# Layer 0's 24 modulation chunks: from products on VectorE to products on TensorE, between the steps of the recurrences

## The chip, the cores and the metric

The kernel runs on one core of a Trainium2 chip. A core has TensorE (matrix products, written PE in the profile, with its weight loads PEld), VectorE (DVE), ScalarE (ACT), GpSimd (POOL) and SyncE (SP), which here issues nearly all transfers, each engine with a program of its own. The metric is the device time of one launch in microseconds; smaller is better.

## The reference

Two layers of a diffusion backbone work on 512 latent tokens of width 1024, with 256 context tokens in layer 0. Per layer, cut to what matters:

```
mod = silu(c) @ ada_w[layer] + ada_b[layer]          # 6 * 1024 values
sh_m, sc_m, gt_m, sh_f, sc_f, gt_f = split(mod, 6)
y = mixer(x * (1 + sc_m) + sh_m)
x = layernorm(4**0.25 * x + gt_m * y)
y = conv_ffn(x * (1 + sc_f) + sh_f)
x = layernorm(4**0.25 * x + gt_f * y)
```

Layer 0's mixer is a gated DeltaNet in both directions with four heads, beside four pooling groups; its results are concatenated and go through one output projection. `mod` is a product of one row with a wide matrix: 24 MB of weights per layer, each used once. Layer 0's `sh_m` and `sc_m` are needed for the first operation of all. The next three vectors, `gt_m`, `sh_f` and `sc_f`, are 3 x 1024 values, or 24 columns of 128: the 24 chunks of the title. They are needed by the output projection's residual (`gt_m`) and by the normalisation behind it (`sh_f`, `sc_f`).

## The kernel before, in words

Activations lie with features on the 128 partitions and tokens along the row. A product in full precision is made of three: weights and activations are split in a high and a low part (`piece`, lines 165 to 179: ScalarE writes `w_hi`, GpSimd or VectorE writes `w_lo`), and `gemm` (line 222) adds high x high, high x low and low x high. A planner fixes each engine's order of instructions ahead of the run, by priorities in program order and by its own estimate of times; an instruction marked `keep_in_program_order` keeps its place among those of its engine.

The first stage (`start`) makes `sh_m` and `sc_m` on TensorE: for each of four groups it loads eight tiles of weights of 128x512, multiplies each with two columns of `silu(c)` and `silu(c_ctx)` as the stationary operand (line 289), into one of four groups of 32 partitions, and turns the sums by four small products with `sel2` (line 311).

`even` then walks through a written plan of steps. `k`, `q` and `v` project keys, queries and values of a pair of heads; `e` sets up systems; `i0` solves the chunk inverses of pair 0, three chains at a time; `x0` runs the two directions of pair 0's recurrence together with the inverses of pair 1, four chains at a time; `r1` runs the recurrence of pair 1; `g`, `p` and `w` are the gates and pools, whose products fill TensorE between the steps of the chains; `d` ends the heads. `together` takes one step of every active chain in turn and may call a function after each turn. Projections take their results in four banks of PSUM (ring "0"), the chains' products in the other four (ring "1").

The 24 chunks are made on VectorE. `ada_rest` (lines 346 to 362) loads, for each column, 128 rows of the transposed weights in two halves of 128x512 (line 356), and multiplies each half with the row `silu(c)`, copied to all partitions, while it sums along the row (line 358). Twelve chunks are done in the turns of x0, eight in those of r1, and the last four in `out_proj`, by `between` (lines 1327 to 1331), one after each output tile; only then does `columns(0)` (line 1285) make the columns for the normalisation. The row of c is loaded and put through Silu once, in the first stage (lines 349 to 351). The feed-forward of layer 0 copies it into two banks (line 580) and makes the other 56 chunks by the same function; these stay as they are.

In `out_proj` the first three output tiles are made in halves of the contraction, as soon as their inputs are there. Tile 3 follows in one piece, and the last four (4 to 7) are made for one half of the tokens and then, in reverse, for the other, with the normalisation of the first half running beside the second.

## Time and profile before

| What | us |
|---|---|
| median of three runs | 1341.77 (1341.52 to 1342.78) |
| the profiled execution's own time | 1340.33 |
| its span | 1338.5 |
| TensorE busy (matmuls) | 1271.3 |
| TensorE busy (weight loads) | 1069.2 |
| VectorE busy | 907.3 |
| GpSimd busy | 680.5 |
| ScalarE busy | 583.9 |

The span runs from the first instruction of the program to the last. Times in the rows count from its start. A row of the timeline has start, duration, engine, line, operation, tiles and form; in square brackets stands how long the engine was idle before it and what ended that. A row of the stretches has the busy time of PE, PEld, DVE, ACT and POOL with the count of instructions, then the granted clock of TensorE as a share of full speed, the busy share of the transfer engines and GB/s. The chain of waits is followed back from the last instruction; its rows are start, duration and what held the time. A row of waits has who waited for whom, the sum in us, how often, and the longest.

### The profile page before, as it was taken

Reading aid. Unit: us, or ns where it says so; the run is one execution under the profiler, and the core shown is the slowest. Engines: PE = TensorE matmul, PEld = TensorE weight load, DVE = VectorE, ACT = ScalarE, POOL = GpSimd, SP = SyncE. Lnnn points to the kernel's source line nnn. Section 1 sums busy time; section 2 is a strip of 40 time slices with the busy share of each in tenths; the row PEclk is TensorE's granted clock in tenths of the full one; section 3 lists DMA queues with packets and bytes.
Section 4 is the critical chain, followed back from the end, with each engine's and each line's share of the span. In section 5 each row is a group of like instructions: output and inputs, shape, how many; then the busy total and the mean of one; then the engine's idle time right before and its main releaser. Section 6 shows DMA issues by size and latency. Waiting matters only on the chain.

```text
span 1338.5 us, 19585 instructions
## 1 busy us (share of the span) xinstructions
PE 1271.3 (95%) x6690; PEld 1069.2 (80%) x6690; DVE 907.3 (68%) x1865; ACT 583.9 (44%) x1091; POOL 680.5 (51%) x616
## 2 busy tenths in 40 slices
PE   6898899989889999999999999999999999999997
PEld 2587777878688888888888988778988888888886
DVE  3397899999776787788644668956676666661125
ACT  2355414445547433333322576545463334332235
POOL 1336447666445665555444566966143433443453
PEclk8899999999988999999999999999899999999998
DMA  9521221522523555656566432323123323333344
GB/s 302 201 87 46 42 60 53 166 83 87 173 81 105 163 189 190 198 194 196 185 206 195 141 111 87 95 87 107 35 95 99 98 95 96 101 91 96 93 123 126
DMA packets 104948, 166.59 MB, mean 124 GB/s; under 512 B 20944, under 2 KB 29200, under 8 KB 104848
## 3 DMA queue, kind: packets, MB, share of 16 engines
q1 hardware_dynamic: 93888, 164.09, 39.2%
q10 hardware_dynamic: 10960, 1.25, 0.7%
q8 instruction: 53, 0.87, 0.3%
q14 instruction: 47, 0.39, 0.1%
HBM read 162.60 MB, written 2.69 MB: 123 GB/s over the span
## 4 chain that ended last, share of the span: by engine, by line
PE 73%; DVE 11%; POOL 4%; issue 3%; ACT 2%; DMA 2%; SPq 0%; ACTq 0%; POOLq 0%; DVEq 0%
PE prod_ps L222 37%; PE out_ps L222 22%; PE half_ps L222 3%; DVE ada_w L358 2%; POOL w_lo L176 1%; PE qkv_ps L222 1%; POOL conf_far L1221 1%; PE ln_e L413 1%; PE it_ps L987 1%; PE gate_ps L222 1%; PE dd_ps L862 1%; DVE x_t L933 1%; DMA ada_w<-in_ada 1%; POOL cb_t L886 1%; PE ln_w L423 1%
## 5 line engine op out<-in xcount | busy, mean ns | idle before, releaser
L176 POOL TENSOR_TENSOR w_lo<-w_raw,w_hi 128x512 fp32r<-128x512 f32 (+1 forms) x299 | 385.0, 1292 | 449.8 <-ACT w_hi L170 441.5
L170 ACT CAST w_hi<-w_raw 128x512 fp32r<-128x512 f32 (+1 forms) x408 | 246.2, 608 | 454.1 <-PE out_ps L222 149.8
L222 PE MATMUL prod_ps<-uh,w_lo 128*128 128x512 f32 x792 | 308.9, 390 | 2.6 <-POOL w_lo L176 2.6
L222 PE MATMUL prod_ps<-uh,w_hi 128*128 128x512 f32 x792 | 308.7, 390 | 0.6 <-ACT w_hi L170 0.6
L222 PE MATMUL prod_ps<-ul,w_hi 128*128 128x512 f32 x792 | 308.4, 389 | 0.0
L601 DVE SCALAR_TENSOR_TENSOR f_acc<-prod_ps,prm,f_acc 128x441 f32<-128x441 f32 (+2 forms) x320 | 222.4, 695 | 60.1 <-ACT f_acc L590 50.8
L176 DVE TENSOR_TENSOR w_lo<-w_raw,w_hi 128x512 fp32r<-128x512 f32 (+1 forms) x109 | 87.0, 799 | 137.7 <-ACT w_hi L170 135.1
L222 PEld LDWEIGHTS prod_ps<-uh,w_lo 128*128 128x128 f32 x792 | 148.7, 188 | 35.2 <-POOL w_lo L176 4.3
L222 PEld LDWEIGHTS prod_ps<-uh,w_hi 128*128 128x128 f32 x792 | 148.8, 188 | 31.9 <-ACT w_hi L170 1.5
L222 PEld LDWEIGHTS prod_ps<-ul,w_hi 128*128 128x128 f32 x792 | 148.7, 188 | 30.4
L222 PE MATMUL out_ps<-ah,w_lo 128*128 128x256 f32 (+1 forms) x352 | 119.6, 340 | 5.6 <-DVE w_lo L176 5.6
L222 PE MATMUL out_ps<-ah,w_hi 128*128 128x256 f32 (+1 forms) x352 | 120.0, 341 | 4.6 <-ACT w_hi L170 2.9
L222 PE MATMUL out_ps<-al,w_hi 128*128 128x256 f32 (+1 forms) x352 | 120.5, 342 | 0.0
L222 PE MATMUL out_ps<-hl,w_hi 128*128 128x512 f32 (+1 forms) x280 | 98.3, 351 | 0.0
L222 PE MATMUL out_ps<-hh,w_hi 128*128 128x512 f32 (+1 forms) x280 | 98.0, 350 | 0.0
L222 PE MATMUL out_ps<-hh,w_lo 128*128 128x512 f32 (+1 forms) x280 | 98.0, 350 | 0.0
L222 PEld LDWEIGHTS out_ps<-ah,w_lo 128*128 128x128 f32 x352 | 68.4, 194 | 12.8 <-DVE w_lo L176 5.9
L222 PEld LDWEIGHTS out_ps<-ah,w_hi 128*128 128x128 f32 x352 | 68.5, 195 | 12.2 <-ACT w_hi L170 3.4
L358 DVE SCALAR_TENSOR_TENSOR ada_w<-ada_w,crow_ps 128x512 f32<-128x512 f32 x112 | 70.8, 683 | 8.7 <-DMA ada_w<-in_ada 8.7
L222 PEld LDWEIGHTS out_ps<-al,w_hi 128*128 128x128 f32 x352 | 68.5, 195 | 7.7 <-DVE al L453 0.8
L222 PEld LDWEIGHTS out_ps<-hl,w_hi 128*128 128x128 f32 x280 | 52.7, 188 | 7.7
L222 PEld LDWEIGHTS out_ps<-hh,w_lo 128*128 128x128 f32 x280 | 52.6, 188 | 7.7
(362 smaller groups left out, 2323.4 us busy)
## 6 DMA issues: line engine op xcount, KB each, us to landing
ada_w<-in_ada SPq DMA_DIRECT2D x192, 256.0 KB, 4.0
w_raw<-in_ffn_up SPq DMA_DIRECT2D x176, 256.0 KB, 2.6
w_raw<-in_ffn_down SPq DMA_DIRECT2D x100, 256.0 KB, 2.7
w_raw<-in_even_in SPq DMA_DIRECT2D x40, 256.0 KB, 2.9
w_raw<-in_odd_in SPq DMA_DIRECT2D x40, 256.0 KB, 2.7
w_raw<-in_even_out SPq DMA_DIRECT2D x16, 256.0 KB, 2.8
w_raw<-in_odd_out SPq DMA_DIRECT2D x16, 256.0 KB, 2.8
w_raw<-in_ffn_down SPq DMA_DIRECT2D x20, 128.0 KB, 2.1
```

What stands on the lines that cost most here:

```text
L170: r = nc.scalar.copy(out=hi[:, :n], in_=raw)
L176: r = eng.tensor_tensor(out=lo[:, :n], in0=raw, in1=hi[:, :n].bitcast(F32), op=SUB)
L222: r = nc.tensor.matmul(out=o, lhsT=w, rhs=x[k][:, c0:c1], start=clear and k == i == 0, stop=k == n - 1 and i == 2, skip_group_check=pin)
L358: r = nc.vector.scalar_tensor_tensor(out=w, in0=w, scalar=1.0, in1=c, op0=MUL, op1=MUL, accum_out=self.mod[:, k, i:i + 1])
L413: nc.tensor.matmul(out=pe[:, 2 * (n * e + i):2 * (n * e + i) + 2], lhsT=t[:, i * P:(i + 1) * P], rhs=ones, start=e == 0 and i == 0 and not ...
L423: nc.tensor.matmul(out=o, lhsT=self.ones, rhs=d[:, 0:n].rearrange("p a b -> p (a b)"), start=True, stop=True)
L601: nc.vector.scalar_tensor_tensor(out=o, in0=sv[:, r0 + dr:r1 + dr, q0 + dc:q1 + dc], scalar=w[:, tap:tap + 1], in1=o, op0=MUL, op1=ADD)
L862: nc.tensor.matmul(out=o, lhsT=self.tri[:, 2 + d], rhs=r, start=d == 0, stop=d == 1)
L886: nc.gpsimd.tensor_tensor(out=t, in0=m[:, 2 * c:2 * c + 2], in1=self.mask(self.blk, 2), op=MUL)
L933: nc.vector.tensor_tensor(out=t, in0=a2[w, :, r, r + 1:16][:, :, None, :].broadcast_to([96, 2, m, m]), in1=x[w, :, r + 1:16, r + 1:16].rea ...
L987: nc.tensor.matmul(out=pt[:, h], lhsT=m[:, h], rhs=r1[:, h], start=True, stop=True)
L1221: nc.gpsimd.tensor_tensor(out=far, in0=far, in1=f, op=ADD)
```

## The change

The 24 chunks are taken out of `ada_rest` and made on TensorE, as in the first stage. The weights for them are laid out in memory as six groups of 512 outputs, each with eight tiles of 128x512 for the contraction (`ada2`). A call of `ada_quad` loads four tiles and multiplies each with a stationary operand of six columns, of which one holds `silu(c)` and five are zero: group g's column stands at place g, so that all six groups add into the same bank, at rows 32q to 32q+5 for the tile's place q among four. Twelve calls make all sums. They are made at every third turn of the chains in i0, x0 and r1, each product kept at its place in TensorE's program. `ada_columns`, a new meaning of the step `a0`, which now stands before `w3 d0 w1 d1`, copies the bank to SBUF, turns and sums it by four small products with `sel6`, and adds the biases. `columns(0)` is called before the output projection, which has no `between` any more. The row of c is loaded at the start of the feed-forward, and its Silu writes the two banks directly. The tag `ada` has six buffers instead of four.

```diff
-PLAN = '... p3 w0 g3 w3 d0 w1 d1 a20'
+PLAN = '... p3 w0 g3 a0 w3 d0 w1 d1'
-ADE = 1
+NG = 6
-AX0 = 12
-AX1 = 8
+ADA_EVERY = 3
-            oo=8, osq=1, ada=4)
+            oo=8, osq=1, ada=6)
...
+        nc.gpsimd.memset(self.csz, 0.0)
+        nc.gpsimd.tensor_copy(out=self.csz[:, :, NG:NG + 1], in_=cs[:, :, 0:1])
...
-        if self.ada_next == 0:
-            nc.sync.dma_start(out=self.crow, in_=self.a["crow"].broadcast_to([P, D]))
-            nc.scalar.activation(out=self.crow, in_=self.crow, func=AF.Silu)
...
+    def ada_quad(self):
+        nc = self.nc
+        n = self.quad
+        if n == 2 * NG:
+            return
+        self.quad += 1
+        if n == 0:
+            self.ada_ps = self.mm("ada_ps")
+            nc.vector.memset(self.ada_ps, 0.0)
+        g, k0 = n // 2, 4 * (n % 2)
+        ws = []
+        for k in range(k0, k0 + 4):
+            ws.append(self.ada_tile(k))
+            nc.sync.dma_start(out=ws[-1], in_=self.a["ada2"][g, :, k])
+        for q, w in enumerate(ws):
+            r = nc.tensor.matmul(out=self.ada_ps[32 * q:32 * q + NG, :], lhsT=self.csz[:, k0 + q, NG - g:2 * NG - g], rhs=w,
+                                 start=n == 0, stop=n == 2 * NG - 1, skip_group_check=True)
+            self.tc.keep_in_program_order(r)
+
+    def ada_columns(self):
+        nc = self.nc
+        while self.quad < 2 * NG:
+            self.ada_quad()
+        rows = self.big("ada_rows")[:, 0:T]
+        nc.scalar.copy(out=rows, in_=self.ada_ps)
+        pt = self.gd("ada_t")
+        for j in range(4):
+            nc.tensor.matmul(out=pt[:, NG * j:NG * j + NG], lhsT=rows[:, j * P:(j + 1) * P], rhs=self.sel6,
+                             start=True, stop=True)
+        nc.vector.tensor_tensor(out=self.mod0.rearrange("p (g j) -> p j g", j=4),
+                                in0=pt[:, 0:4 * NG].rearrange("p (j g) -> p j g", g=NG),
+                                in1=self.mbias[:, 0:24].rearrange("p (g j) -> p j g", j=4), op=ADD)
...
+                crow = fp.tile([P, D], F32, name="crow")
+                nc.sync.dma_start(out=crow, in_=self.a["crow"].broadcast_to([P, D]))
                 for k, o in enumerate(self.crow_ps):
-                    nc.scalar.copy(out=o, in_=self.crow[:, T * k:T * k + T])
+                    nc.scalar.activation(out=o, in_=crow[:, T * k:T * k + T], func=AF.Silu)
...
-            def each(i):
-                def f():
-                    if left[0][i] and self.ada_next < 24:
-                        left[0][i] -= 1
-                        self.ada_rest(1, True)
-                return f
+            turns = [0]
+            def each():
+                turns[0] += 1
+                if turns[0] % ADA_EVERY == 0:
+                    self.ada_quad()
...
-                i=lambda p: together(self.inverses(p, ps[p]), NI),
-                r=lambda p: together(self.recurrence(p, ps[p]), 2, each(1)),
-                x=lambda p: together(self.recurrence(0, ps[0]) + self.inverses(1, ps[1]), NX, each(0)),
+                i=lambda p: together(self.inverses(p, ps[p]), NI, each),
+                r=lambda p: together(self.recurrence(p, ps[p]), 2, each),
+                x=lambda p: together(self.recurrence(0, ps[0]) + self.inverses(1, ps[1]), NX, each),
...
-                a=lambda n: self.ada_rest(n - self.ada_next, True),
+                a=lambda n: self.ada_columns(),
...
-        self.gt_m0 = self.mods(0, 8, "mod_g")
+        self.gt_m0 = self.mod0[:, 0:8]
+        self.columns(0)
...
-            def between(m):
-                if self.ada_next < 24:
-                    self.ada_rest(min(ADE, 24 - self.ada_next))
-                    if self.ada_next >= 24:
-                        self.columns(0)
...
-                          ahead=AHEAD, ring=ring, between=between,
+                          ahead=AHEAD, ring=ring,
```

More of the change, by code (lines that the diff above doesn't have):

```diff
@@ L36 @@
 PARAM_SHAPES = (
-    ("ident", (P,)), ("sel2", (2,)), ("mb0", (16,)), ("gconv", (12, 5)), ("alog", (8,)), ("dtb", (8,)), ("ev", (3,)),
+    ("ident", (P,)), ("sel2", (2,)), ("sel6", (6,)), ("mb0", (16,)), ("gconv", (12, 5)), ("alog", (8,)), ("dtb", (8,)), ("ev", (3,)),
     ("mbias", (80,)), ("lng", (4, KD)), ("lnb", (4, KD)), ("sconv", (4, 3)),
@@ L43 @@
                ("id16", (16,)), ("up16", (16,)), ("low16", (16,)))
-PLAN = 'b0 k0 k1 e0 q0 n0 e1 q1 v0 g0 i0 n1 v1 g1 x0 p0 p1 r1 p2 g2 w2 p3 w0 g3 w3 d0 w1 d1 a20'
+PLAN = 'b0 k0 k1 e0 q0 n0 e1 q1 v0 g0 i0 n1 v1 g1 x0 p0 p1 r1 p2 g2 w2 p3 w0 g3 a0 w3 d0 w1 d1'
 NI = 3
@@ L153, in constants @@
         self.mod = cp.tile([P, 2, 80], F32, name="mod")
-        self.ada_next = 0
+        self.mod0 = cp.tile([P, 24], F32, name="mod0")
+        self.csz = cp.tile([P, KD, 2 * NG], F32, name="csz")
+        self.quad = 0
+        self.ada_next = 24
         self.crow_ps = None
-        self.crow = cp.tile([P, D], F32, name="crow")
     def raw(self, src):
@@ L355, in ada_rest @@
                 cs = slice(T * k, T * k + T)
-                nc.sync.dma_start(out=w, in_=self.a["ada1"][i][:, cs])
-                c = self.crow_ps[k] if self.crow_ps else self.crow[:, cs]
-                r = nc.vector.scalar_tensor_tensor(out=w, in0=w, scalar=1.0, in1=c, op0=MUL, op1=MUL,
+                nc.sync.dma_start(out=w, in_=self.a["ada1"][i - 24][:, cs])
+                r = nc.vector.scalar_tensor_tensor(out=w, in0=w, scalar=1.0, in1=self.crow_ps[k], op0=MUL, op1=MUL,
                                                    accum_out=self.mod[:, k, i:i + 1])
@@ L639, in even @@
             ps, pooled, self.decays = {}, [], {}
-            left = [[AX0, AX1]]
-            def each(i):
-                def f():
-                    if left[0][i] and self.ada_next < 24:
-                        left[0][i] -= 1
-                        self.ada_rest(1, True)
-                return f
+            turns = [0]
[3 more added lines that the diff above has]
+                    self.ada_quad()
             steps = dict(
@@ L1285, in columns @@
         if part == 0:
-            m = self.mods(8, 16, "mod_0")
-            self.cols[0] = self.modulation(0, m[:, 0:8], m[:, 8:16], "f0")
+            m = self.mod0
+            self.cols[0] = self.modulation(0, m[:, 8:16], m[:, 16:24], "f0")
         if part == 1:
@@ L1322, in run @@
             nc.scalar.activation(out=self.zs[k], in_=self.zs[k], func=AF.Copy, scale=ALPHA)
-        self.gt_m0 = self.mods(0, 8, "mod_g")
+        self.gt_m0 = self.mod0[:, 0:8]
+        self.columns(0)
         with ExitStack() as ctx:
             ap = self.pool("ada", ctx=ctx)
-            self.ada_tile = lambda k: ap.tile([P, T], F32, tag="ada", bufs=6, name="ada_w")
-            def between(m):
-                if self.ada_next < 24:
-                    self.ada_rest(min(ADE, 24 - self.ada_next))
-                    if self.ada_next >= 24:
-                        self.columns(0)
             ring = lambda nm: ap.tile([P, T], F32R, tag="w", bufs=4 * LAST[0], name=nm)
             self.out_proj(a["even_out"], KD, self.ah, self.al, self.gt_m0, 0, self.uh, self.ul,
-                          ahead=AHEAD, ring=ring, between=between,
+                          ahead=AHEAD, ring=ring,
                           first=[a["ffn_up"][0, i * KF] for i in range(READY[0])])
@@ L1378, in layout @@
     d["ada0"] = cc(np.concatenate([sh, sc], -1).transpose(2, 1, 0, 3))
-    d["ada1"] = cc(np.concatenate([w0[:, 2 * D:], w1], 1).T.reshape(80, P, D))
+    d["ada2"] = cc(w0[:, 2 * D:5 * D].reshape(KD, P, NG, T).transpose(2, 1, 0, 3))
+    d["ada1"] = cc(np.concatenate([w0[:, 5 * D:], w1], 1).T.reshape(56, P, D))
     d["even_in"] = tiles(f["even_w_in"][:, :2560])
@@ L1403, in layout @@
     sel = np.zeros((P, 2), one)
+    sel6 = np.zeros((P, NG), one)
     for q in range(4):
+        sel6[32 * q:32 * q + NG] = np.eye(NG)
         sel[32 * q, 0] = sel[32 * q + 1, 1] = 1
     v = dict(
-        ident=i == j, sel2=sel, mb0=cols(f["ada_b"][0, :2 * D]),
+        ident=i == j, sel2=sel, sel6=sel6, mb0=cols(f["ada_b"][0, :2 * D]),
         gconv=f["gdn_conv_w"].T.reshape(12, P, 5).transpose(1, 0, 2), alog=wide(f["gdn_a_log"]),
```

## The prediction

> **What bounds the kernel now.** I read the page first, then the busy time by stretches around the change, the chain of waits there, TensorE's waits, and last the timeline of the output projection, engine by engine.
>
> ```profile
> span 1338.5 us, 19585 instructions
> ...
> PE 73%; DVE 11%; POOL 4%; issue 3%; ACT 2%; DMA 2%; SPq 0%; ACTq 0%; POOLq 0%; DVEq 0%
> ```
>
> Over the whole span the chain that ends last is TensorE for 73% and VectorE for 11%. The old work of the 24 chunks lies between 226 and 371 us, so only that part is asked further. By stretches (busy us of PE, PEld, DVE, ACT, POOL with instruction counts, then TensorE's granted clock): the inverses of pair 0 with the value projections, the shared stretch x0, the first part of r1, the rest of r1.
>
> ```profile
> 176.00:222.00 46.00, 41.75 (x274) 35.57 (x275) 43.42 (x102) 13.86 (x34) 27.92 (x36) 1.00 0.14 32
> 222.00:292.00 70.00, 66.11 (x460) 57.45 (x459) 65.27 (x179) 27.61 (x81) 48.33 (x54) 1.00 0.38 121
> 292.00:316.00 24.00, 20.50 (x131) 17.12 (x131) 23.13 (x71) 14.57 (x44) 13.56 (x15) 1.00 0.52 154
> 316.00:336.00 20.00, 19.90 (x138) 17.70 (x138) 17.76 (x57) 10.45 (x28) 13.87 (x14) 1.00 0.08 27
> ```
>
> VectorE is 93 to 96% busy in the first three. TensorE's matmul time is nearly as full, but weight loads, which leave the gaps visible, fill 57.45 of 70 us (82%), 17.12 of 24 (71%) and 17.70 of 20 (88.5%). So the recurrences have two nearly full engines. What the 20 chunks there take of VectorE (line 358 alone):
>
> ```profile
> 222.00:292.00 70.00, 22.36 (x50) 1.00 0.38 121
> 292.00:316.00 24.00, 13.13 (x30) 1.00 0.52 154
> ```
>
> That is 35.5 us of the 88.4 that VectorE is busy. The chain of 222 to 336 us shows how much of it sets the time, then how much TensorE waited in the second and third stretch:
>
> ```profile
> by line: DVE ada_w L358 13.4%; PE it_ps L987 7.0%; PE pool_ps L222 6.8%; PE v_ps L1082 6.4%; PE gate_ps L222 6.3%; PE k_ps L1072 6.1%; issue 5.8%; PE o_ps L1105 5.0%; PE v_ps L1090 4.8%; PE o_ps L1108 4.7%; PE iv_ps L995 4.0%; DVE r L980 3.
> ...
> 307.48 3.12 DMA ada_w<-in_ada
> 331.69 4.13 PE gate_ps L222 x18
> ```
>
> ```profile
> PE it_ps L987 <- DVE r L980: 0.8, 2, 0.4
> PE it_ps L987 <- DVE r L1005: 0.7, 2, 0.6
> PE o_ps L1105 <- DVE s L1096: 0.7, 1, 0.7
> PE iv_ps L1002 <- DVE g L1000: 0.6, 2, 0.4
> PE k_ps L1060 <- ACT g L998: 0.4, 1, 0.4
> ...
> PE k_ps L1072 <- DVE s L1093: 2.3, 1, 2.3
> PE k_ps L1060 <- DVE oo L1116: 0.8, 1, 0.8
> PE k_ps L1072 <- DVE s L1096: 0.7, 1, 0.7
> ```
>
> On the chain the chunks hold 13.4% of 114 us = 15.3 us, and one of their loads 3.1 us. Yet TensorE's waits that the view lists add up to 3.2 + 3.8 = 7.0 us only: while VectorE works at the chunks, TensorE mostly has projections (pool, gate) to fill in, and it still has eighteen gate products left at 331.69. This gap, 18.4 on the chain against 7.0 waited, decides most of what follows.
>
> The plainest loss is in the output projection, with the last four chunks:
>
> ```profile
> 349.10 3.65 SPq L1321 DMA_DIRECT2D z<-in_xT  x8
> 352.79 9.66 SPq L356 DMA_DIRECT2D ada_w<-in_ada  x8
> 362.54 12.37 SPq L162 DMA_DIRECT2D w_raw<-in_even_out  x8
> ...
> 363.45 0.39 PE L222 MATMUL out_ps<-ah,w_lo 128*128 128x512 f32 x1
> 366.77 0.58 PE L222 MATMUL out_ps<-ah,w_hi 128*128 128x256 f32 x1 [2.93 <-ACT w_hi L170]
> 373.19 0.58 PE L222 MATMUL out_ps<-ah,w_lo 128*128 128x256 f32 x1 [5.62 <-DVE w_lo L176]
> ...
> 368.94 1.74 DVE L358 SCALAR_TENSOR_TENSOR ada_w<-ada_w,crow 128x512 f32<-128x512 f32 x1
> 372.44 0.69 DVE L176 TENSOR_TENSOR w_lo<-w_raw,w_hi 128x512 fp32r<-128x512 f32 x1
> ```
>
> The weights of output tile 4 are issued behind eight chunk loads on SP's queue, so TensorE waits 2.93 us for them; then their low half stands behind the chunks' products on VectorE, and TensorE waits 5.62 us more.
>
> **The change part by part.**
>
> *Out of the output projection.* With no chunk there, both waits lose their cause: 2.93 + 5.62 = 8.55 us. The clock follows:
>
> ```profile
> 373.00:377.00 4.00, 3.81 (x18) 3.82 (x19) 1.39 (x3) 1.83 (x3) 3.06 (x3) 0.52 0.67 208
> 377.00:380.00 3.00, 3.00 (x27) 3.00 (x27) 2.17 (x4) 1.49 (x4) 2.45 (x3) 1.00 0.48 150
> ...
> z<-in_xT SPq DMA_DIRECT2D x8, 256.0 KB, 5.7
> ```
>
> After the wait TensorE does 18 matmuls in 4 us at a clock of 0.52, then 27 in 3 us at 1.00; the 18 would take 2 us at the later rate, so 1.9 us more go (the first starts at 373.19). The Trainium skill, "TensorE: Matmul & The Clock Gate", section "What's actually happening", says the array falls to half clock after an idle window of some 3.4 us and needs about as long busy to come back; the trace agrees with its 3.7 slow us. What is late next: the same weights, now behind the eight z loads only. These are issued from 349.10 to 352.75 and land 5.7 us after issue in the median, so by about 359; the weights follow, and TensorE wants them at 363.7. with 0.69 for the split (row 372.44) and about as much for the cast, I estimate 3 us of slack. I take -10.4; bounds -5 (half of it comes back as a wait for these weights) and -11.5.
>
> *Into the recurrences.* The code's turns: six inverses of six turns each, three at a time, make 12 in i0; x0 and r1 have 19 each. At every third turn, that is 4 quads in i0, 6 in x0, 2 in r1. The price of a quad stands in the first stage, where the same four products with two columns instead of six go to the same four partition groups:
>
> ```profile
> 25.31 1.04 PE L289 MATMUL ada_ps<-ada_w,cs 128*2 128x512 f32 x8
> 26.28 0.50 PE L222 MATMUL qkv_ps<-ah,w_hi 128*128 128x512 f32 x1
> ```
>
> The trace has two records for one such product (64 for the 32 of the first stage), so the eight are one quad: 26.28 - 25.31 = 0.97 us. Twelve cost 11.6 us of TensorE, against 48 products on VectorE that cost 35.5 us for the first 40.
>
> In x0 and r1, eight quads add 7.8 us. Against them stands what VectorE gives back. If only the listed waits go: -7.0, net +0.8. If TensorE reaches in all three stretches the density of the last one, where the chain is nothing but TensorE: (57.45 + 17.12 + 17.70) / 0.885 = 104.3, plus 7.8 = 112.1 of 114 us, net -1.9. If all that lies on the chain goes: -18.4 + 7.8 = -10.6. If nothing goes: +7.8. I take -1, near the two middle ones, because the projections have to be computed in any case and TensorE has little room.
>
> In i0, four quads cost 3.9 us. They lie beside VectorE, busy for 43.42 of 46 us, while weight loads leave TensorE 10.4 us; between 0 and +3.9 I take +1, as each quad stands in the row between two steps of a chain.
>
> *The bank.* The accumulator takes one of the four banks of the projections from the third turn of i0 until a0. The value projections of pair 1 need four results at once, each emptied by VectorE, which is the late engine there. At worst one projection (24 products of 4.13 / 18 = 0.229 us) moves out of i0's free time: +5.5; at best none. I take +1.5.
>
> *The columns at a0.* One ScalarE copy, four small products and one VectorE addition, in a part where TensorE sets the time: four products of the first stage's kind, with the transposed rows, are eight records at about 0.11 us, less than one quad; the rest lies beside the gate products. +0.3, bounds 0 and +1. `columns(0)` moves with it, from VectorE at 371 us to before the projection, where VectorE has time.
>
> *The loads.* The same 48 loads of 256 KB; eight leave SP's queue at 352.79 (counted), the others now stand between the value and gate weights. With six buffers, four loads and half of the next quad's are ahead; the other two wait for the quad before.
>
> *The row of c.* It is loaded and put through Silu at the start of the feed-forward instead of in the first stage. There it lay beside VectorE's work, so nothing is gained. Where it goes:
>
> ```profile
> 400.41 0.81 SPq L356 DMA_DIRECT2D ada_w<-in_ada  x2
> 402.49 0.33 SPq L162 DMA_DIRECT2D w_raw<-in_ffn_up  x1
> ...
> 407.90 0.58 ACT L580 COPY crow_ps<-crow 128x512 f32<-128x512 f32 x1
> 429.46 1.28 ACT L603 ACT_TABLE_LOAD   x1 [0.16 <-DVE f_acc L601]
> ...
> crow<-in_crow SPq DMA_DIRECT2D x1, 512.0 KB, 7.0
> ```
>
> The new load is 512 KB, took 7.0 us before, and stands ahead of the next weights; behind it on ScalarE stand the casts of weights and of the normalised rows. Silu needs a table load of 1.28 us that now comes once at 429.46; if it falls ahead of the square root of the second half, there are two more. Between 0 and +4 I take +1, as the results are wanted only after 440 us.
>
> *Sum:* -10.4 - 1 + 1 + 1.5 + 0.3 + 1 = -7.6 us. The profiled execution took 1340.33 us (1.8 beside its span); it becomes 1332.7. The median of the runs shown, 1341.77, lies 1.44 above the profiled one, so the forecast is **1334.2**.
>
> **Rivals.**
>
> *VectorE was the bound.* If the chain is right and its 18.4 us go, the recurrences give -10.6 instead of -1: 1324.6. For it: VectorE at 93 to 96%. Against it: 7.0 us of listed waits, and gate products left over at the end.
>
> *TensorE was the bound already (slower).* The quads then are pure addition in all three steps: 11.6 in place of -1 + 1, so -10.4 + 11.6 + 1.5 + 0.3 + 1 = +4.0: 1345.8. It decides once less than 11.6 + 2.8 - 10.4 = 4.0 us of waits come back. For it: the matmul rows nearly touch. Against it: weight loads at 71 and 82%, where 88.5% has been shown.
>
> *The wait stays in the output projection*, now behind z: half of 10.4, 1339.4. Against it: the 3 us of slack.
>
> *The quads' loads are late.* A quad waits with everything behind it on TensorE, so a late load stalls the chains too. Landing takes a median of 4.0 us, three turns of x0 take 70 / 19 x 3 = 11 us, so this needs SP's queue to stand still behind a weight load. At 1.5 us for each of 12 quads: +18, 1352.
>
> ```profile
> ada_w<-in_ada SPq DMA_DIRECT2D x192, 256.0 KB, 4.0
> ```
>
> **How the numbers follow.** Forecast 0.50, VectorE bound 0.20, TensorE bound 0.13, wait stays 0.11, late loads 0.06. The forecast's own range, from its unknowns (bank, row of c, recurrences), is 1329 to 1339. For 8 in 10 I reach into VectorE's case and to the third rival: 1325 to 1341. This kernel's runs can tell about 0.2% (2.7 us) from no change. Faster by more than that: forecast, VectorE's case and a part of the third, 0.76; within it 0.10; slower 0.14, from TensorE's case and the late loads.
>
> **What would show it.** No wait over 1 us and no clock below 1.00 between 345 and 375 us; quads of about 0.97 us with no DMA wait before them; weight loads at 85% or more in x0; VectorE below 75% there; the Silu of the row after the second square root. I am wrong if the end of the recurrences moves by more than 6 us either way, or if the projection still waits for its fifth tile's weights.

## The result and the profile after

The changed kernel takes 1348.62 us (median of 5 runs, 1346.15 to 1351.59) against 1341.77 us (1339.44 to 1343.29) for the kernel before in the same runs: ratio 1.0052, 95% interval 1.0033 to 1.0071. It is slower by about 7 us, where 7.6 us were to be gained; the forecast was 1334.2 and the range ended at 1341.

The profiled execution took 1348.45 us, with a span of 1346.7. Line numbers of the changed kernel differ from those of before; the names of the tiles are the same. The page's shares of the chain that ends last:

```profile
span 1346.7 us, 19664 instructions
...
PE 75%; DVE 8%; POOL 5%; ACT 3%; issue 2%; DMA 2%; SPq 0%; ACTq 0%; POOLq 0%; DVEq 0%
```

VectorE's share fell from 11% to 8%, as the change intends, and the span grew by 8.2 us. To find where, I cut the span at starts of certain products in the trace:

| stretch | before | after | difference |
|---|---|---|---|
| start to the first projection product behind the last kk | 141.0 | 139.2 | -1.8 |
| from there to the last gate product | 194.4 | 201.8 | +7.4 |
| last gate product to the first of the output projection | 3.6 | 10.2 | +6.5 |
| first to last product of the output projection | 61.0 | 58.4 | -2.7 |
| from there to the first product of the feed-forward | 0.9 | 4.6 | +3.6 |
| the feed-forward's first products, by halves | 24.9 | 22.0 | -2.9 |
| all the rest | 912.5 | 910.6 | -1.9 |

Two rows carry the growth: the recurrences (I call the second row "the recurrence part") and the gap behind the last gate. The output projection, which was to give back 10.4 us, gave 2.7. The first and last rows explain nothing: kernels below that have the changed kernel's code in these two places take 138.8 to 142.8 us and 908.9 to 915.2.

The recurrence part by one row of the stretch view for each kernel (busy us of PE, PEld, DVE, ACT, POOL, then the clock). Before:

```profile
141.00:335.60 194.60, 178.93 (x1164) 155.11 (x1163) 179.28 (x473) 79.48 (x204) 119.98 (x135) 0.98 0.29 84
```

After:

```profile
139.20:341.20 202.00, 189.33 (x1260) 157.69 (x1259) 143.68 (x395) 80.90 (x208) 105.97 (x133) 0.98 0.30 89
```

VectorE lost 35.6 us, almost exactly the 35.5 of the prediction. TensorE gained 96 records, the 12 quads, and 10.4 busy us; the stretch became 7.4 us longer. The matmul time was 92% before (178.93 of 194.60) and 94% after: what TensorE did not do, 15.7 us, shrank by 3.0 only.

A finer cut of the changed kernel shows the chains early and the projections late:

```profile
222.00:287.00 65.00, 64.28 (x485) 54.11 (x484) 46.30 (x137) 27.20 (x81) 33.30 (x46) 1.00 0.35 114
287.00:310.00 23.00, 21.52 (x146) 16.92 (x145) 10.52 (x35) 11.78 (x40) 11.65 (x15) 1.00 0.31 98
...
325.00:341.00 16.00, 16.00 (x68) 12.48 (x67) 5.83 (x19) 10.60 (x19) 8.09 (x7) 1.00 0.21 67
```

The last product of the recurrences starts at 324.8 us, 6.6 earlier than before (331.4), but the fourth pooling projection and the last gate are still to come: before, the pooling was through at 321.6 and only gate products were left; now it ends at 334.7. In 325 to 341 TensorE is busy all 16.00 us, with weight loads for 12.48, which is 78%.

Then the gap. TensorE from the last gate product on:

```profile
341.04 0.39 PE L224 MATMUL gate_ps<-ah,w_lo 128*128 128x512 f32 x1
341.26 0.95 PE L395 MATMUL ada_t<-prm,ada_rows 128*128 128x6 f32 x8
345.95 2.07 PE L1220 MATMUL pool_y<-pool_o,even_k 128*128 128x512 f32 x2 [3.73 <-DVE pool_o L1214]
347.81 1.92 PE L1179 MATMUL ot_ps<-prm,oo 128*128 128x128 f32 x8
349.52 1.50 PE L1220 MATMUL pool_y<-pool_o,even_k 128*128 128x512 f32 x2
350.86 0.60 PE L1179 MATMUL ot_ps<-prm,oo 128*128 128x128 f32 x4
351.21 0.48 PE L224 MATMUL out_ps<-ah,w_hi 128*128 128x512 f32 x1
```

The pooling's own product waits 3.73 us, and the first pair of its kind then takes 2.07 us and not about 1: the granted clock was 0.50 from 343.6 to 350.4. What it waits for, on GpSimd and then on VectorE:

```profile
336.88 1.06 POOL L1205 TENSOR_TENSOR pool_q<-pool_b 128x527 f32<-128x527 f32 x1
338.02 2.20 POOL L1205 TENSOR_TENSOR pool_q<-pool_q 128x525 f32<-128x525 f32 x2
340.17 1.30 POOL L490 TENSOR_TENSOR al<-pool_o,ah 128x512 fp32r<-128x512 f32 x1
341.42 1.28 POOL L1205 TENSOR_TENSOR pool_q<-pool_q 128x513 f32<-128x513 f32 x1
...
342.74 1.74 DVE L1209 SCALAR_TENSOR_TENSOR pool_o<-pool_q,pool_b 128x512 f32<-128x512 f32 x1 [7.85 <-POOL pool_q L1205]
344.51 1.18 DVE L1213 TENSOR_TENSOR pool_o<-pool_q,prm 128x8 f32<-128x8 f32 x2
345.65 0.24 DVE L1214 TENSOR_TENSOR pool_o<-pool_o,pool_b 128x8 f32<-128x8 f32 x2
```

Four window sums, a split queued among them, and three steps on VectorE (five instructions): nine us from 336.88 to 345.9, which a projection that ended 14 us earlier had hidden.

In the output projection the waits for the fifth tile's weights are gone, as forecast. In their place:

```profile
383.66 1.29 POOL L434 TENSOR_TENSOR ln_s<-ln_s,z 128x512 f32<-128x512 f32 x1
384.91 1.26 POOL L178 TENSOR_TENSOR w_lo<-w_raw,w_hi 128x512 fp32r<-128x512 f32 x1
386.14 1.44 POOL L437 TENSOR_TENSOR ln_s<-ln_s,ln_sq 128x512 f32<-128x512 f32 x1
...
384.98 1.48 DVE L434 TENSOR_TENSOR ln_s<-ln_s,z 128x256 f32<-128x256 f32 x1 [4.30 <-POOL ln_s L434]
...
390.40 1.83 PE L450 MATMUL ln_e<-onesn,ln_s 128*128 128x2 f32 x8 [4.85 <-DVE ln_s L434]
```

The sums for the normalisation run through GpSimd, whose queue holds weight splits, then through VectorE, where the first took 1.48 us and the next of its kind, at 388.47, 0.42; TensorE waits 4.85 us for them, and the clock is at 0.50 from 388.0 to 401.7. So the half clock that was to go is there too.

The quads themselves are as priced: eight records in 1.04 us, the next product 0.97 us after, no wait on a load.

```profile
195.09 1.04 PE L382 MATMUL ada_ps<-ada_w,csz 128*6 128x512 f32 x8
196.06 0.44 PE L1039 MATMUL iv_ps<-prm,g 128*128 128x128 f32 x2
```

### The profile page after: what moved, and what is told of

Same layout as the page of the kernel before. It is cut to its first block, busy times and chain, and to the rows that moved or that the text cites. A ratio compares the mean times of both kernels' runs of the same rounds, so it can differ in the third digit from the quotient of the medians.

```text
span 1346.7 us, 19664 instructions
## 1 busy us (share of the span) xinstructions
PE 1283.4 (95%) x6794; PEld 1075.2 (80%) x6794; DVE 858.5 (64%) x1767; ACT 583.9 (43%) x1091; POOL 668.8 (50%) x618
## 4 chain that ended last, share of the span: by engine, by line
PE 75%; DVE 8%; POOL 5%; ACT 3%; issue 2%; DMA 2%; SPq 0%; ACTq 0%; POOLq 0%; DVEq 0%
PE prod_ps L224 37%; PE out_ps L224 21%; PE half_ps L224 3%; PE qkv_ps L224 1%; POOL w_lo L178 1%; PE ln_e L450 1%; PE pool_ps L224 1%; PE it_ps L1024 1%; PE iv_ps L1032 1%; POOL conf_far L1258 1%; DVE x_t L970 1%; PE dd_ps L899 1%; PE gate_ps L224 1%; PE ada_ps L382 1%; PE ln_w L460 1%
```

## The experiments

Unless it says otherwise each is the changed kernel with the edit shown; ratios are against the kernel before, with their 95% intervals. For the changed kernel that ratio is 1.0052.

**The accumulator in the chains' ring of banks.**

```diff
-            self.ada_ps = self.mm("ada_ps")
+            self.ada_ps = self.gd("ada_ps")
```

> One edit to the changed kernel: the accumulator of the quads takes a bank of the chains' four instead of the projections' four. Marks of the changed kernel: the last product of the value projections starts at 220 us (203 before), the first product of the output projection at 351.2 (339.1 before). Theory A (the lost bank): the value projections end near 203 to 207 again, the output projection starts 5 to 9 us earlier than 351, and the launch is 5 to 8 us shorter than the changed kernel's 1348.6. Theory B (TensorE was full, the 11.6 us of quads are pure addition): the value projections may move, but the output projection starts within 2 us of 351, since the same products have to be done; launch 1346 to 1350. If the chains need their fourth bank, both are wrong and it is later than 351.

Measured 1350.24 us, 1.0069 (1.0046 to 1.0092). The fourth value projection of pair 1 ended at 199.8 us again (before 202.7, changed 220.1), but the recurrence part took 203.6 us and the output projection began at 353.8. Giving the projections their bank back gained nothing in the end. As it takes a bank from the chains, this run alone doesn't price a bank.

**The quads left out, the bank held.** The columns hold their biases alone.

```diff
-        for k in range(k0, k0 + 4):
+        for k in ():
```

> The changed kernel without the quads' 48 loads and products; the accumulator is set to zero and holds its bank as before, so the 24 columns hold the biases alone: that part of the computation is left out. Theory B (quads are pure addition): the output projection starts up to 11.6 us earlier, near 340, launch near 1337 to 1340. Theory A (the lost bank): the bank is still lost, so the start moves by no more than 4 us, launch 1344 to 1348. Either way TensorE's work in x0 without VectorE's products is seen: weight loads above 85% there if TensorE is the bound.

Measured 1347.14 us, 1.0044 (1.0028 to 1.006). The recurrence part fell to 199.3 us only. This looked like a bank that costs 5 us, but the clock was at half for 10.2 us between 203 and 296 us, where the changed kernel's was full, and half a clock for 10.2 us can cost up to 5.1; so it decides little by itself. The gap behind the last gate stayed at 9.7 us.

**More of the output projection's splits on VectorE.**

```diff
-SHARE_OUT = (0.35, 0.5)
+SHARE_OUT = (0.7, 0.5)
```

> One edit to the changed kernel: in layer 0's output projection 70% instead of 35% of the low halves of the weights are made by VectorE, the rest by GpSimd. In the changed kernel TensorE waits there 4.85 us for the first sum of the normalisation, which stands behind low halves on GpSimd, and 2.0 us for a square, and runs at half clock for 13.7 us from 388. Theory G (the wait went from VectorE and the loads to GpSimd's queue): the 4.85 us wait goes, the clock stays at 1.00 from 351 to 405, the time from the first output product to the first feed-forward product falls from 62.9 to 52 to 56 us, and the launch is 6 to 10 us shorter than 1348.6. Rival (it waits for loads or for the products themselves): 61 to 64 us between these marks, launch unchanged within 2 us.

Measured 1352.18 us, 1.0079 (1.0061 to 1.0098). The output projection to the first feed-forward product fell from 62.9 to 56.3 us, next to the 52 to 56 that the theory of GpSimd's queue named; but the rest took 919.4 us in place of 910.6. The share is a running fraction, and a shifted fraction hands other splits of the second layer to VectorE and GpSimd; TensorE there waits 3.9 us once for a split on VectorE.

**All quads before the recurrences**, between the keys and the inverses of pair 0 (twelve steps in the order written out, the columns there too).

```diff
-PLAN = 'b0 k0 k1 e0 q0 n0 e1 q1 v0 g0 i0 n1 v1 g1 x0 p0 p1 r1 p2 g2 w2 p3 w0 g3 a0 w3 d0 w1 d1'
+PLAN = 'b0 k0 u0 k1 u0 u0 e0 u0 u0 q0 u0 n0 e1 u0 u0 q1 u0 u0 v0 u0 g0 u0 a0 i0 n1 v1 g1 x0 p0 p1 r1 p2 g2 w2 p3 w0 g3 w3 d0 w1 d1'
+                u=lambda n: self.ada_quad(),
```

> The changed kernel with the same twelve quads called between the earlier steps of the plan (one or two after each of k0 to g0), and their columns made ahead of i0, so that the bank is free again for i0, x0 and r1 and no quad stands among the chains. Theory B (TensorE full in x0 and r1): the first output product comes at 339.1 - 18 + 2 to 4 for what the quads cost in the early steps, so 324 to 332, and the launch is 1328 to 1336. Theory A says the same for the part of the bank alone, about 5 to 9 us of 12: start at 342 to 346, launch near 1340. If the early steps are as full as x0, the quads only move: start near 351. The wait in the output projection is untouched, 62 to 63 us from the first output product to the first feed-forward product.

Measured 1367.56 us, 1.0214 (1.0182 to 1.0247). The recurrence part began 13.8 us later, its last gate came 20.0 us later, and the part, whose last quad now stands at 204.6 us and none in the shared stretch or behind it, took 208.0 us. None of the cases expected fits: the quads were to gain there, or at worst to move, and cost more than among the chains. Why the early part is so dear isn't shown.

**Neither quads nor bank.** The columns are the biases, so the products of the modulation are left out; VectorE has no chunks, TensorE no quads.

```diff
                 if turns[0] % ADA_EVERY == 0:
-                    self.ada_quad()
+                    pass
 ...
-        while self.quad < 2 * NG:
-            self.ada_quad()
 ...
+        nc.vector.tensor_copy(out=self.mod0, in_=self.mbias[:, 0:24])
```

> The changed kernel without the quads, their loads and their accumulator: the 24 columns hold their biases alone, so the products of the modulation are left out; VectorE has no chunks, TensorE no quads, the projections have all four banks. Bank theory (the accumulator's bank is what made the projections late): the fourth value projection of pair 1 ends near 203 us again, as before, the first product of the output projection comes at 339 us or earlier (before 339.1, after 351.2), and the time is 1333 us or less. Order theory (once VectorE has no chunks the chains' products come ahead in TensorE's order and the pool and gate projections are left to the end, whatever the banks): the value projection ends near 203 us, yet the first product of the output projection comes at 344 us or later and the time is 1340 us or more.

Measured 1342.79 us, 0.9996 (0.9977 to 1.0015), no faster than before. Its recurrence part:

```profile
142.20:336.10 193.90, 178.30 (x1164) 156.54 (x1162) 146.07 (x394) 79.91 (x207) 106.64 (x133) 0.97 0.13 36
```

This is the most telling row of the study. VectorE is rid of 33 us of work, nothing is added to TensorE, and the stretch is 0.7 us shorter than before: with the same 1164 products, TensorE is just as busy (178.30) and idle (15.6). The chains were quicker (the inverses end at 277.2, before 290.1), and the projections came that much later. Where the chains' small products prevail TensorE is nearly full, and then it waits again:

```profile
223.00:280.00 57.00, 55.65 (x428) 51.12 (x427) 45.93 (x132) 24.82 (x78) 33.91 (x46) 1.00 0.08 25
...
304.00:320.80 16.80, 13.46 (x95) 12.61 (x94) 9.36 (x34) 4.55 (x14) 8.20 (x12) 0.90 0.02 7
...
306.87 1.27 DVE L1199 SCALAR_TENSOR_TENSOR pool_o<-pool_q,pool_b 128x512 f32<-128x512 f32 x1 [2.91 <-POOL pool_q L1195]
...
308.58 0.59 DVE L1123 SCALAR_TENSOR_TENSOR s<-s,gc_ex,v_ps 128x128 f32<-128x128 f32 x2
...
309.06 0.46 PE L1099 MATMUL k_ps<-s,kl 128*128 128x128 f32 x2 [3.34 <-DVE s L1123]
```

TensorE waits 3.34 us for a step `s` of the chain on VectorE, though VectorE has no chunk and has itself been idle for 2.91 us: its order puts a step of the pooling first, which waits for GpSimd. So a wait that the view puts down to VectorE can come from the order of its instructions and not from its load. The order theory holds, in this form: TensorE's work, with the waits that its order has anyway, was the bound, and VectorE's freedom mostly changes which of it comes first. Whether another order of the chains and the pooling would take these waits out, no run here shows. The gap behind the last gate is 11.6 us here too, so quads don't cause it.

**The fourth pooling projection ahead of the last two gates.**

```diff
-... p0 p1 r1 p2 g2 w2 p3 w0 g3 a0 w3 d0 w1 d1'
+... p0 p1 r1 p2 p3 g2 w2 w0 g3 a0 w3 d0 w1 d1'
```

> The changed kernel with the fourth pooling projection written ahead of the third and fourth gates, so that what is left to TensorE after the recurrences are gates, not the pooling with its GpSimd and VectorE tail. Tail theory (part of the 12.1 us by which the output projection starts later is the tail of the fourth pooling, 3.7 us waited for its VectorE step and what is queued around it): the first product of the output projection comes 3 to 6 us earlier than 351.2 and the time is 1343 to 1346 us. Pure-addition theory (TensorE is full with quads up to there, and nothing waits that matters): it stays within 1.5 us of 351.2 and the time at 1347 to 1350 us.

Measured 1339.63 us, 0.9986 (0.9968 to 1.0004): level with the kernel before. The gap fell from 10.2 to 4.1 us, and the output projection took 54.1 us in place of 58.4, with half clock for 3.4 us of it in place of 13.7. The recurrence part stayed (202.6). The first output product came only 1.7 us earlier than in the changed kernel, at 349.5, as everything ahead of the recurrence part took 3.6 us more in this profile.

**The kernel before, its last four chunks moved from the output projection into the second recurrence.**

```diff
-PLAN = '... w1 d1 a20'
+PLAN = '... w1 d1 a24'
 ...
-AX1 = 8
+AX1 = 12
 ...
         self.gt_m0 = self.mods(0, 8, "mod_g")
+        self.columns(0)
```

> The kernel before, with its last four chunks on VectorE inside the second recurrence (12 and 12 in place of 12 and 8) and the columns made before the output projection: no chunk in the output projection, no quad, no accumulator. My prediction's term by itself: the output projection to the first feed-forward product, 61.9 us before, falls by 5 to 11.5 us; the recurrences end 0 to 4 us later; time 1332 to 1338 us. Rival (the halves of the output projection are held by the weight splits and sums on GpSimd anyway, as in the changed kernel, where this stretch took 62.9 us): the stretch stays within 2 us of 61.9 and the time at 1341 to 1345 us.

Measured 1342.83 us, 1.0011 (0.9996 to 1.0026). This prices two things apart. The output projection with no chunk in it took 59.7 us in place of 61.0, not ten less: the wait had moved to the sums.

```profile
385.53 1.84 PE L413 MATMUL ln_e<-onesn,ln_s 128*128 128x2 f32 x8 [3.87 <-DVE ln_s L397]
```

And four chunks more on VectorE, 8.5 us more of its busy time in the part, made the recurrence part 7.6 us longer (3.4 us of it, from 333.4, are at half clock):

```profile
139.10:341.30 202.20, 181.52 (x1164) 156.55 (x1163) 187.81 (x488) 79.26 (x202) 121.63 (x135) 0.97 0.31 90
```

Beside the row without any chunks this says that the two engines were balanced: more on VectorE costs about its length, less gains next to nothing.

**The splits on VectorE again, with the running fraction put back afterwards** (a second counter runs with 0.35 and is copied back at the end of the projection).

> The changed kernel with 70% in place of 35% of the output projection's weight splits on VectorE, and the alternation of the splits put back afterwards to where it would have stood, so that the later stages split as in the changed kernel. Queue theory (the wait of 4.85 us and the half clock in the output projection come from splits queued on GpSimd ahead of the sums; the 8.9 us that the same edit lost later came from the shifted alternation): the output projection to the first feed-forward product takes 55 to 58 us in place of 62.9, the rest stays within 2 us of 910.5, and the time is 1341 to 1344 us. Rival (the late loss belongs to the edit itself or to the instruction order): the rest takes 915 us or more again and the time is 1347 us or more.

Measured 1342.31 us, 1.0006 (0.999 to 1.0023). The late loss is gone (the rest took 910.6 us), so it was the fraction; the output projection to the feed-forward took 59.0 us, a little over what was expected.

**Both: pooling first, and the splits.**

> The changed kernel with two of the edits together: the fourth pooling projection ahead of the third and fourth gates, and 70% of the output projection's splits on VectorE with the alternation put back afterwards. Theory of two separate places (the pooling tail ahead of the output projection, 6 us, and GpSimd's queue inside it, 4 us): the last gate to the first output product takes 4 us in place of 10.2, the output projection to the first feed-forward product 55 to 57 us in place of 62.9, and the time is 1334 to 1338 us. Rival (both edits relieve the same wait, so that they don't add up): the output projection stays at 58.7 us or more, as with either alone, and the time at 1339 to 1342 us.

Measured 1336.68 us (1332.24 to 1339.54), 0.9961 (0.9948 to 0.9974): faster than both kernels. The gap is 4.1 us, and the output projection:

```profile
348.30:398.60 50.30, 49.02 (x317) 44.02 (x315) 32.83 (x69) 26.39 (x50) 20.84 (x16) 1.00 0.36 117
```

50.3 us with the clock at 1.00 throughout, against 61.1 before and 58.5 in the changed kernel:

```profile
339.10:400.20 61.10, 50.90 (x314) 45.51 (x313) 43.52 (x88) 28.47 (x55) 29.00 (x21) 0.92 0.41 134
```

```profile
351.20:409.70 58.50, 53.65 (x316) 49.08 (x315) 27.58 (x62) 26.88 (x51) 28.22 (x21) 0.88 0.31 99
```

The 10.4 us of the prediction were there to be had, but only once the next two waits were removed too. With the splits alone the first to the last output product took 54.8 us, with 10.2 us at half clock; why the slow clock doesn't set in when the pooling is ahead as well isn't shown.

**Quads from the shared stretch on only** (every second turn), so that the bank is taken later.

```diff
-ADA_EVERY = 3
+ADA_EVERY = 2
 ...
-                i=lambda p: together(self.inverses(p, ps[p]), NI, each),
+                i=lambda p: together(self.inverses(p, ps[p]), NI),
```

> The changed kernel with no quad in the inverses of pair 0: the quads start in the shared stretch, at every second turn, nine there and three in the second recurrence; so the accumulator takes its bank some 40 us later. Bank theory (without the quads but with the bank held, the part from the last kk product to the last gate took 199.3 us; without both 193.7; with both 201.8): the fourth value projection of pair 1 ends near 203 us after a start like that of before, and the part takes 196 to 199 us in place of 201.8; time 1343 to 1346 us. Rival (the bank costs as much wherever it is held, since the shared stretch needs four as well): the part stays at 201 us or more, time 1347 us or more.

Measured 1347.5 us, 1.0044 (1.0027 to 1.0061). The value projection ended at 202.5 us, yet the recurrence part took 202.5 us: no gain.

**All three edits.**

> All three edits together: quads from the shared stretch on, the fourth pooling projection ahead of the last two gates, 70% of the output projection's splits on VectorE with the alternation put back. If the three places are separate: 1330 to 1335 us, faster than the kernel before. If the bank costs the same wherever it is held: 1335 to 1339 us.

Measured 1336.47 us, 0.9967 (0.9955 to 0.998): the same as without the later start.

**The row of c in its old place**, with four buffers for the chunks.

```diff
+            nc.sync.dma_start(out=self.crow, in_=self.a["crow"].broadcast_to([P, D]))   # at the first quad
+            nc.scalar.activation(out=self.crow, in_=self.crow, func=AF.Silu)
 ...
-                    nc.scalar.activation(out=o, in_=crow[:, T * k:T * k + T], func=AF.Silu)
+                    nc.scalar.copy(out=o, in_=self.crow[:, T * k:T * k + T])
```

> The changed kernel with the row of c loaded and put through Silu at the first quad and copied at the start of the feed-forward, as the kernel before did it, with four chunk buffers in place of six, which makes room for the row. Theory that the moved row costs about 1 us: the last output product to the first feed-forward product falls from 4.5 us to about 1, the first feed-forward products take some 25 us in place of 22, and the time is 1346 to 1348 us. Rival (the new load and the table loads cost 3 us or more): that stretch falls and the feed-forward's first products stay at 22 us, time 1345 us or less. If four buffers leave quads waiting for their loads, the part from the last kk product to the last gate grows by 2 us or more.

Measured 1346.15 us, 1.0042 (1.0025 to 1.0059). From the last output product to the first whole feed-forward product it took 0.48 + 24.86 = 25.34 us, against 4.57 + 22.00 = 26.57 in the changed kernel. It looks as if the move costs 1.2 us there, by the table loads that it brings:

```profile
413.51 1.28 ACT L619 ACT_TABLE_LOAD   x1
414.81 0.60 ACT L619 ACTIVATE crow_ps<-crow 128x512 f32<-128x512 f32 x1
415.43 1.28 ACT L480 ACT_TABLE_LOAD   x1
416.72 0.29 ACT L480 ACTIVATE ln_q<-ln_q,eps 128x2 f32<-128x2 f32 x1
```

These are ScalarE's instructions of the changed kernel: the Silu of the first bank falls ahead of the second half's square root, that of the second bank behind it, and two table loads more come with that. But the other kernels don't bear the price out. In seven of those here with the row in its new place (the bank in the chains' ring, the quads left out, all quads early, the splits with the fraction put back, the later start, the last two of this section) the same two stretches took 25.3 to 25.4 us, as with the row in its old place; in the seven others, the changed kernel among them, 26.6. The eight at 25.3 to 25.4 had 3.4 us of half clock there, the seven at 26.6 had 6.8. So the 1.2 us go with the slow clock, and a cost of the moved row isn't shown.

**Every quad issued twice**, from the same loads (the columns hold twice the products).

```diff
-        for q, w in enumerate(ws):
+        for z in range(2):
+            for q, w in enumerate(ws):
 ...
```

> The changed kernel with every quad's four products issued twice into the accumulator, from the same loads (the columns hold twice the products, so the result is another). Addition theory (TensorE has no room there, quads are added as they are): the part from the last kk product to the last gate grows from 201.8 us by 8 to 12 us, time 1356 to 1361 us. Bank theory (the quads cost 2.5 us for all twelve, the bank 5.6): it grows by 1 to 4 us, time 1350 to 1353 us.

Measured 1353.85 us, 1.0089 (1.0066 to 1.0112). The recurrence part:

```profile
139.55:352.10 212.55, 199.59 (x1356) 160.22 (x1355) 143.36 (x395) 79.54 (x207) 105.17 (x133) 0.98 0.29 85
```

96 more records, 10.3 us more of busy TensorE, 10.55 us more of time, at the same length of half clock (6.8 us in either). That is addition. The whole, 5.2 us longer, lies between what the two theories expected and so decides nothing: the output projection and the stages behind it had less slow clock this time.

**The bank from the shared stretch on, without quads.**

> The kernel whose quads start in the shared stretch, without the quads and their loads: the accumulator holds its bank from the shared stretch on and nothing is added to it; the columns hold their biases alone. Addition theory: the part from the last kk product to the last gate takes 193 to 196 us, as with neither quads nor bank (193.7), against 202.5 with the quads. Bank theory: 198 to 202 us.

Measured 1340.0 us, 0.999 (0.9973 to 1.0007). The recurrence part:

```profile
140.45:333.10 192.65, 179.15 (x1164) 158.49 (x1163) 143.52 (x395) 80.62 (x208) 106.02 (x133) 0.96 0.14 36
```

As short as without the bank (193.90): held there, the bank costs nothing that shows.

**Neither quads nor bank, with the pooling first.**

> The kernel with neither quads, loads of quads nor accumulator (columns of biases alone), with the fourth pooling projection ahead of the third and fourth gates. If the order written out kept the gain of VectorE's freedom back: the last kk product to the last gate stays near 194 us, the last gate to the first output product falls from 11.5 to 4 us, and the time is 1332 to 1336 us. If VectorE's freedom were worth the 7 us of listed waits or more once the order is better: the part to the last gate falls to 187 us or less and the time to 1329 us or less.

Measured 1332.47 us, 0.9931 (0.9911 to 0.9951). The recurrence part, and the gap 3.2 us:

```profile
141.30:333.00 191.70, 177.18 (x1164) 156.34 (x1163) 149.86 (x400) 78.32 (x206) 109.55 (x135) 0.97 0.13 36
```

Even with the work of the chunks gone from every engine the part is 2.8 us shorter than before and does not come near 187: in this order the 7 us of listed waits were not to be had by taking chunks from VectorE.

## Why the prediction was wrong

The forecast missed the span by 15.8 us: +8.2 in place of -7.6. By the table three steps failed. The output projection gave 7.7 us less than forecast, the gap behind the last gate, which the sum doesn't have, took 6.5, and the recurrences with the quads were 5.6 dearer. The row of c came out 0.3 better, and the first and last rows, which nothing explains, 3.7.

*The recurrences.* The step that failed is "Into the recurrences", in the sentence that takes the weight loads as the view that leaves the gaps visible, and from it "TensorE reaches in all three stretches the density of the last one". I read 82% of weight loads in the shared stretch as 18% of room, with 88.5% as the mark of a full engine. But the share depends on what is multiplied. Where the changed kernel's TensorE does almost nothing but projections, busy 16.00 of 16.00 us, the loads fill 78%; in the kernel without chunks they reach 90% in the shared stretch (51.12 of 57 us), where the chains' small products prevail. So 82% was no gap. The matmul time, which I set aside as nearly as full, was the better guide: 92% over the part. In the second and third stretch it left TensorE idle for 3.9 + 3.5 = 7.4 us, which agrees with the 7.0 us of listed waits; the density that I assumed, 104.3 of 114 us, asks for 9.7. The page "Perfetto Trace Analysis" of the Trainium skill, section "Identifying the Most-Contended Engine", says that the share of matmul time is not a good measure of how close TensorE is to its limit, and names the rate of useful work and the share of weight loads in its place; here the measurement went the other way for the share of weight loads.

*The size.* For the quads, the bank and the columns against what VectorE gives back I took -1 + 1 + 1.5 + 0.3 = +1.8; measured were +7.4 (the columns' own products, at 341.26, already lie in the gap behind). By the rows above: chunks off VectorE -0.7, twelve quads +8.1 (202.00 against 193.90) to +9.4 (against 192.65), twelve more +10.55. The price of a quad, 0.97 us, was about right (10.55 us for twelve are 0.88 each); what should have come back for it did not. That is the rival "TensorE was the bound already", which I gave 0.13 because of the same 82%. It named +11.6, the upper end. That its 1345.8 lies only 2.8 us from the measured time is luck: its sum kept the -10.4 of the output projection and had no gap. The -0.7 for the chunks has 3.4 us of half clock in it that the kernel before didn't have there, so VectorE's freedom may be worth up to 2.4 us, near the 2.8 of the last experiment; either is far from what the chunks took on VectorE.

*A term that was missing*, put at nothing without a reason: the order of what is left at the end, +6.5 us. The prediction used the eighteen gate products at 331.69 as a sign that TensorE had work left, but did not ask which work would be left when the chains got ahead. It was the pooling, which has a tail of nine us on GpSimd and VectorE; with gates left to the end the gap is 3 to 4 us. The edit that puts the pooling first took 6.1 us of it back. That the kernel with neither quads nor bank has the gap too shows that the faster chains bring it, not the quads.

*The output projection*: -10.4 forecast, -2.7 measured, -1.3 with the chunks moved out of the kernel before. Of this step, right: the two waits went, and the weights of the fifth tile did come in time behind the z loads. The step that failed is the one from "with no chunk there, both waits lose their cause" to counting them whole. I asked what is late next on SP's queue and found slack, and did not ask it of GpSimd, which works almost without a break from 375 to 387 us and through which the sums go that TensorE needs. The bound of -5 was still too good. With the sums' queue relieved and the gap gone, the whole 10.8 us appeared (61.1 to 50.3); so this was a gain held back, not a gain that did not exist.

*The bank*: +1.5 taken. Held from the shared stretch on it costs nothing measurable. The value projection did move out of the inverses, as the bound had it (202.7 to 220.1), but freeing it there gained nothing either. What the bank costs when it is held from the inverses on with no quads is open, since that one run had the half clock in it.

*The row of c*: +1 taken; +0.7 by the two stretches of the changed kernel against the kernel before. The two table loads that I named as a possibility did come, but with equal lengths of half clock nothing is left of the difference to the row in its old place.

*The loads of the quads*: never late in the changed kernel, as expected. Where quads stand closer together (all early, or at every second turn) single quads did wait for a load, 0.50 us at most.

*Of the signs* that I listed: the quads and VectorE's share in the shared stretch (46.30 of 65 us, 71%) came as told; the absence of waits and of slow clock from 345 to 375 us (3.73 us and 0.50 stood there), the weight loads at 85% (54.11 of 65 us, 83%) and the Silu behind the second square root did not (its first half came ahead). The sign of being wrong by the end of the recurrences came too: their last product moved by 6.6 us.

Not explained: the -1.8 us ahead of the recurrence part and the -1.9 in all the rest. The rest of the kernel took 908.9 to 915.2 us in the runs that left its code and its split order alone, with the slow-clock stretches at other places each time. So a single profile can't tell differences below some 3 us between whole spans, and the verdicts above rest on the timed rounds and on the short stretches.

## What to carry to other kernels

Before work is moved from one engine to another, take the work away without putting it anywhere: the row of the kernel with neither chunks nor quads would have shown in one run that there was next to nothing to gain in the recurrences, in the order as it was written. Don't read the free room of TensorE from the share of weight loads unless the mix of shapes stays the same; compare a stretch of the same shapes that is known to be full. And when chains get faster, look at what is left over at the end: leave the work with the shortest tail for last, and follow the wait that you remove through every queue that feeds the next product, GpSimd's too.

## What the runs showed of the hardware

The half clock comes in pieces of 3.4 us: 3.4, 6.8, 10.2 and 13.7 us in all these traces, but for the last one, which the end of the program cuts. In the changed kernel it began within the wait of 3.73 us behind the last gate and lasted 6.8 us; it began within the wait of 4.85 us in the output projection and lasted, with the smaller gaps that followed, 13.7. In the kernel before it began, at 366.6, within the wait of 2.93 us already and lasted 10.2. So such a wait costs more than its length: the two products of the pooling that took 2.07 us behind it took 1.10 in the kernel with the pooling first.

A weight split on VectorE took 0.69 us, but some took far longer. In the kernel with both edits, beside a busy GpSimd:

```profile
373.07 3.09 DVE L180 TENSOR_TENSOR w_lo<-w_raw,w_hi 128x512 fp32r<-128x512 f32 x2 [0.32 <-ACT w_hi L172]
...
373.87 1.74 POOL L180 TENSOR_TENSOR w_lo<-w_raw,w_hi 128x512 fp32r<-128x512 f32 x1
```

That is 1.55 us each on VectorE, and 1.74 on GpSimd against 1.29 elsewhere. Over this whole trace, the 64 splits of this shape on VectorE beside which GpSimd did nothing took 0.69 us at most; the 34 that ran beside GpSimd for 0.3 us or more took 1.11 in the median and up to 1.78. The Trainium skill's page "SBUF — State Buffer", section "Who interferes with whom", says that a VectorE instruction with two inputs in SBUF contends with a GpSimd instruction that reads SBUF; these rows agree. So a split handed from GpSimd to VectorE can cost well over 0.69 us there when GpSimd stays busy beside it.
